# Linear attention in a fixed order, with paired products, gate products in between, and reordered weight loads

## The chip, the cores and the metric

The kernel runs on one core of one Trainium2 chip. The metric is the device time of one execution in microseconds (us); lower is better. A core has TensorE (PE, matmul; PEld is its weight load), VectorE (DVE), ScalarE (ACT), GpSimd (POOL), and SyncE (SP), whose queue issues all the loads that are spoken of here. Loads go from HBM into SBUF over 16 DMA engines; matmul results land in PSUM.

## What is computed

Two transformer blocks over 256 tokens of width 1024. The change lies in the first block, between its input projections and the routing of its mixture of experts (MoE). The part that matters of the reference:

```python
# two-directional gated linear attention: 4 heads, key width 128, value width 256, chunks of 64 tokens
cum = jnp.cumsum(la, axis=3); last = cum[:, :, :, -1:, :]
q_dec = qc * jnp.exp(cum); k_inv = kc * jnp.exp(-cum); k_rem = kc * jnp.exp(last - cum)
scores = jnp.where(lower, jnp.einsum('bhnid,bhnjd->bhnij', q_dec, k_inv), 0.0)
o_intra = jnp.einsum('bhnij,bhnjv->bhniv', scores, vc)
def step(state, inp):
    q_n, k_n, v_n, d_n = inp
    o_n = jnp.einsum('bhid,bhdv->bhiv', q_n, state)
    state = d_n[..., None] * state + jnp.einsum('bhid,bhiv->bhdv', k_n, v_n)
    return state, o_n
# forward, and backward over the flipped sequence; the start states come from a second sequence, ctx
ox = o_f + flip(o_b)
# mixer
o = _rmsnorm(o, gla_onorm_g)
y_gla = jnp.matmul(o * jax.nn.silu(g), w_gla_br)     # g: 1024 columns of the input projection w_in
gate_pool, gate_gla = jnp.split(jax.nn.sigmoid(gates), 2, axis=-1)
x = x + g1 * jnp.matmul(gate_pool * y_pool + gate_gla * y_gla, w_o)
# then 32 experts, two per token; then the second block (two attentions, two MLPs)
x = x + g2 * _hier_moe(...)
```

## The kernel before

The core works through the stages one after the other: projections of x and ctx, linear attention, the mixer with its gates, routing, the MoE with 192 weight tiles of 1 MB each, and the second block. Each dense product against a float32 weight is made of three products of split operands. `Chunk` loads a chunk of 1024 rows by 512 columns as two tiles of 1 MB (line 125) into a ring of three buffers named `raw`. `split` turns each chunk into four pieces `wsp`: ScalarE copies the high part (L243), VectorE subtracts it (L244). `mmB` then issues, for each group of 128 tokens (m), 24 matmuls of 512 columns (L283 to L285), so 48 for a chunk. There are four `wsp` buffers, so a chunk's piece is written when the last product on the former chunk's piece is done.

The linear attention is the loop `for hp in range(2)` over pairs of heads. For each pair it makes
- the start states of both directions from ctx (`krc` by `vc`, L578), copied by VectorE into `SS` (L581), which is the buffer F[4],
- the products inside the chunks (`scT` by `vx`, L587) into two PSUM tiles `po` with the tag "mm", of which there are four buffers,
- four steps. In each, for direction d, chunk n (n = step forward, 3 − step backward): the query product `qdec` by state `Sb(d, h)` (L596), with 64 output rows, which go to the upper or the lower half of a PSUM tile; the key-value product `krx` by `vx` (L603), which contracts over 64 rows; and the update of the state by VectorE (L607). Both directions' chunks lie in different halves of the 128 rows in every step. The last step has no key-value product and no update,
- the squares (L612, ScalarE), the root (L614, L166 to L176), and the scaling into `og` (L619, VectorE).

The chunk of `w_in` for g has two halves of 512 columns, called gate halves below. The loop `for h in range(2)` makes them; each half ends in a sigmoid (L153 to L155), a product by VectorE (L707) and one by GpSimd (L708). After them come the pool projection u, four chunks for `gates`, and the rest of the mixer.

Small products of the modulation vector ride along: `adaln_chunk` (L195) multiplies 1024 rows of `w_mod`, loaded by `wm_load` (L690) into buffers that are free by then (FA, XA, F[0], F[4]), in four column groups of 32; `adaln_T` (L213) and `adaln_bc` (L222) spread the result. `wm[4]` stands in FA and XA, `wm[5]` in F[0] and F[4].

`W.load` (L664) issues MoE tiles ahead. The first of them go into a pool "ring2" of seven buffers that lies where the work tiles of the attention (pool `fg`) were, so it must wait until these are done with.

The order on each engine: instructions outside of an `in_order` region are placed by a scheduler that simulates the engines; inside one, TensorE, ScalarE and VectorE keep the order of the code among themselves. From `sp.enter_context` on, SP's queue keeps the order of the code, too. Each engine works its own queue in order, and an instruction that waits holds up all behind it.

Of the kernel before, what the change touches and what calls it, by code (L numbers as in the profile page):

```python
# [13 lines left out]
AF = mybir.ActivationFunctionType  # L14
# [3 lines left out]
P = 128  # L18
# [3 lines left out]
NT = 2  # L22
# [65 lines left out]
def build(tc, I, out, dbg=None):  # L88
# [8 lines left out]
    with ExitStack() as top:  # L97
# [7 lines left out]
        def PS(tag="ps"):  # L105
            return psum.tile([P, 512], F32, name=tag, tag=tag)
# [243 lines left out]
        with b1:  # L350
# [217 lines left out]

            oss = fg.tile([P, 2, NT, 2], F32, name="oss")
            ors = fg.tile([P, 2, NT, 2], F32, name="ors")  # L570
            og = f3(F[2])
            for hp in range(2):
# [9 lines left out]
                po = []  # L582
                for m in range(NT):
                    po.append(PS("mm"))
                    for hh in range(2):
                        h = 2 * hp + hh
                        nc.tensor.matmul(po[m][:, hh * 256:(hh + 1) * 256], scT[0][m][:, h], vx[m][:, h * 256:(h + 1) * 256],  # L587
                                         start=(hh == 0), stop=False, skip_group_check=True)
                for step in range(4):
                    for d in range(2):  # L590
                        n = step if d == 0 else 3 - step
                        m, r = n // 2, n % 2
                        rsl = slice(64 * r, 64 * r + 64)
                        for hh in range(2):
                            h = 2 * hp + hh
                            nc.tensor.matmul(po[m][rsl, hh * 256:(hh + 1) * 256], qdec[d][:, h, n * 64:n * 64 + 64], Sb(d, h),  # L596
                                             start=False, stop=False, tile_position=(0, 64 * r), skip_group_check=True)
                        if step == 3:
                            continue
                        pkv = PS()  # L600
                        for hh in range(2):
                            h = 2 * hp + hh
                            nc.tensor.matmul(pkv[:, hh * 256:(hh + 1) * 256], krx[m][d][rsl, h * P:(h + 1) * P],  # L603
                                             vx[m][rsl, h * 256:(h + 1) * 256], start=True, stop=True, skip_group_check=True)
                        for hh in range(2):
                            h = 2 * hp + hh
                            nc.vector.scalar_tensor_tensor(Sb(d, h), Sb(d, h), dec[:, d, h, n:n + 1],  # L607
                                                           pkv[:, hh * 256:(hh + 1) * 256], op0=OP.mult, op1=OP.add)
                for m in range(NT):
                    for hh in range(2):  # L610
                        junk = fg.tile([P, 256], F32, name="aff", tag="aff", bufs=3)
                        nc.scalar.activation(junk, po[m][:, hh * 256:(hh + 1) * 256], AF.Square, accum_out=oss[:, hp, m, hh:hh + 1])  # L612
# [3 lines left out]
                for m in range(NT):  # L616
                    for hh in range(2):
                        h = 2 * hp + hh
                        nc.vector.tensor_scalar(og[:, m, h * 256:(h + 1) * 256], po[m][:, hh * 256:(hh + 1) * 256],  # L619
                                                ors[:, hp, m, hh:hh + 1], None, op0=OP.mult)  # L620

# [74 lines left out]
            for h in range(2):  # L696
                wg = Chunk(w_in, 2560 + h * 512)
                wm[4 + h] = wm_load(4 + h, *((FA, XA[0], XA[1]), (F[0], F[4]))[h])
                W.load(1)
                pg = denseC(wg, X)  # L700
# [11 lines left out]
            wg = Chunk(w_in, 0)  # L712
            wm[10] = wm_load(10, FA, F[4])
            W.load(1)
# [18 lines left out]
            for i in range(4):  # L733
# [3 lines left out]
                W.load(1)  # L737
# [977 lines left out]
```

## Time and profile before

| | us |
|---|---|
| median of three runs | 1460.36 (1458.88 to 1462.91) |
| the profiled execution | 1460.49 |
| its span in the profile | 1458.7 |
| TensorE busy in the span | 1275.9 (87%) |
| all MoE tiles | 192 loads of 1 MB |

The span leaves 1.8 us of the profiled execution outside. The profile has a row of tenths for each engine in 40 slices of 36.5 us, a row for the clock granted to TensorE (9 is nearly the whole of 2.4 GHz, a stretch at 0.5 ran at 1.2 GHz), and the share of the DMA engines. A float32 matmul of the program is two records in the trace, one of float32r is one. The end of a matmul is modelled; the start is measured. A busy TensorE is therefore not one at its peak, and the pitch of starts says more.

### The profile page before, as it was taken

How to read it: one execution, taken by the hardware profiler on the slowest of the kernel's cores; microseconds unless marked ns; L12 is line 12 of the kernel's file. 1: busy time of each engine (PE TensorE's matmuls, PEld its weight loads, DVE VectorE, ACT ScalarE, POOL GpSimd, SP SyncE). 2: the span in 40 equal slices, each digit the busy share in tenths (PEclk: the TensorE clock that was granted, in tenths of full speed). 3: DMA queues.
4: the chain of work that ended last, by engine and by line, in shares of the span. 5: the costliest groups of instructions: out<-in, count | busy, mean ns of one | idle time of the engine just before them, and what ended most of it. 6: DMA issues, size and time to landing. Idle time of an engine off the chain costs nothing.

```text
span 1458.7 us, 17343 instructions
## 1 busy us (share of the span) xinstructions
PE 1275.9 (87%) x7063; PEld 879.3 (60%) x7064; DVE 644.3 (44%) x978; ACT 481.0 (33%) x802; POOL 110.9 (8%) x57
## 2 busy tenths in 40 slices
PE   6899997999987776777777689999999998799997
PEld 4776755787732121221222167878999887688996
DVE  2543233457521120211201078675555765955554
ACT  3443104564410000000000066634445345444441
POOL 1100000000000000000000043030000320600000
PEclk9989998999998898998988899999999999999999
DMA  9822017955899999999999966146565450665650
GB/s 357 307 101 81 36 58 287 373 187 191 352 421 420 421 381 421 421 420 421 421 421 421 415 219 217 58 153 215 181 202 175 172 188 1 203 214 174 202 174 29
DMA packets 112672, 368.82 MB, mean 253 GB/s; under 512 B 7979, under 2 KB 9899, under 8 KB 88012
## 3 DMA queue, kind: packets, MB, share of 16 engines
q1 hardware_dynamic: 112588, 367.67, 66.3%
q8 instruction: 57, 0.93, 0.3%
q14 instruction: 27, 0.22, 0.0%
HBM read 366.60 MB, written 1.05 MB: 252 GB/s over the span
## 4 chain that ended last, share of the span: by engine, by line
PE 32%; DMA 22%; DVE 5%; ACT 2%; issue 1%; POOL 1%; SPq 0%; DVEq 0%; ACTq 0%; POOLq 0%
DMA raw<-in_moe_w_dram 21%; PE mm L285 7%; PE mm L284 6%; PE mm L283 6%; PE ps L299 3%; PE ps L298 3%; PE ps L297 3%; DVE wsp L244 2%; PE mm L1455 1%; DMA raw<-in_moba_w_qkv_dram 1%; DVE x L1318 1%; ACT wsp L243 1%; PE ps L1411 0%; DVE x L1321 0%; PE ps L1260 0%
## 5 line engine op out<-in xcount | busy, mean ns | idle before, releaser
L244 DVE TENSOR_TENSOR wsp<-raw,wsp 128x1024 fp32r<-128x1024 f32 (+1 forms) x208 | 260.5, 1267 | 180.8 <-ACT wsp L243 174.8
L243 ACT ACTIVATE wsp<-raw 128x1024 fp32r<-128x1024 f32 (+1 forms) x234 | 240.6, 1049 | 195.0 <-PE mm L285 69.8
L1057 PE MATMUL mm<-raw,XA 128*32 128x512 f32 x1024 | 190.4, 706 | 76.8 <-DMA raw<-in_moe_w_dram 73.6
L1057 PEld LDWEIGHTS mm<-raw,XA 128*32 128x32 f32 x1024 | 42.9, 125 | 218.8 <-DMA raw<-in_moe_w_dram 135.2
L244 POOL TENSOR_TENSOR wsp<-raw,wsp 128x1024 fp32r<-128x1024 f32 x26 | 65.8, 2553 | 783.1 <-PE ps L1106 469.7
L1073 DVE SCALAR_TENSOR_TENSOR t<-mm,w,t 128x512 f32<-128x512 f32 x8 | 8.9, 1112 | 255.3 <-PE mm L1057 215.3
L1057 PE MATMUL mm<-raw,t 128*32 128x512 f32 x512 | 86.4, 674 | 25.7 <-DMA raw<-in_moe_w_dram 23.3
L298 PE MATMUL ps<-hTl,wsp 128*128 128x256 f32 x384 | 108.7, 283 | 0.0
L299 PE MATMUL ps<-hTh,wsp 128*128 128x256 f32 x384 | 108.7, 283 | 0.0
L297 PE MATMUL ps<-hTh,wsp 128*128 128x256 f32 x384 | 108.6, 283 | 0.0
L283 PE MATMUL mm<-wsp,hh 128*128 128x512 f32 x240 | 93.8, 391 | 0.0
L284 PE MATMUL mm<-wsp,hh 128*128 128x512 f32 x240 | 93.6, 390 | 0.0
L285 PE MATMUL mm<-wsp,hl 128*128 128x512 f32 x240 | 93.3, 390 | 0.0
L284 PE MATMUL mm<-wsp,hTh 128*128 128x512 f32 (+1 forms) x224 | 86.9, 388 | 1.4 <-POOL wsp L244 1.4
L283 PE MATMUL mm<-wsp,hTh 128*128 128x512 f32 (+1 forms) x224 | 87.4, 390 | 0.0
L285 PE MATMUL mm<-wsp,hTl 128*128 128x512 f32 (+1 forms) x224 | 87.0, 389 | 0.0
L283 PE MATMUL mm<-wsp,R1h 128*128 128x512 f32 x176 | 70.8, 410 | 10.7 <-ACT wsp L243 10.7
L297 PEld LDWEIGHTS ps<-hTh,wsp 128*128 128x128 f32 x384 | 73.7, 192 | 0.6
L298 PEld LDWEIGHTS ps<-hTl,wsp 128*128 128x128 f32 x384 | 73.7, 192 | 0.5
L299 PEld LDWEIGHTS ps<-hTh,wsp 128*128 128x128 f32 x384 | 73.7, 192 | 0.1
L1057 PEld LDWEIGHTS mm<-raw,t 128*32 128x32 f32 x512 | 19.7, 121 | 87.3 <-DMA raw<-in_moe_w_dram 42.9
L284 PE MATMUL mm<-wsp,R1h 128*128 128x512 f32 x176 | 70.9, 405 | 1.4 <-DVE wsp L244 1.3
(390 smaller groups left out, 2088.0 us busy)
## 6 DMA issues: line engine op xcount, KB each, us to landing
raw<-in_moe_w_dram SPq DMA_DIRECT2D x192, 1024.0 KB, 19.8
raw<-in_mlp_w_in_dram SPq DMA_DIRECT2D x32, 1024.0 KB, 5.4
raw<-in_mlp_w_out_dram SPq DMA_DIRECT2D x32, 1024.0 KB, 5.3
raw<-in_w_in_dram SPq DMA_DIRECT2D x22, 1024.0 KB, 12.1
F<-in_w_mod_dram SPq DMA_DIRECT2D x16, 1024.0 KB, 11.0
raw<-in_moba_w_qkv_dram SPq DMA_DIRECT2D x12, 1024.0 KB, 7.2
raw<-in_dil_w_qkv_dram SPq DMA_DIRECT2D x8, 1024.0 KB, 5.2
FA<-in_w_mod_dram SPq DMA_DIRECT2D x4, 1024.0 KB, 12.5
```

The costliest lines, as they stand in the source:

```text
L243: nc.scalar.activation(hi, src, AF.Copy)
L244: eng.tensor_tensor(lo, src, hi.bitcast(F32), op=OP.subtract)
L283: nc.tensor.matmul(ps[:, :n], xh[:, k0 + k, sl], hi, start=(first and k == 0), stop=False)
L284: nc.tensor.matmul(ps[:, :n], xh[:, k0 + k, sl], lo, start=False, stop=False)
L285: nc.tensor.matmul(ps[:, :n], xl[:, k0 + k, sl], hi, start=False, stop=(last and k == e))
L297: nc.tensor.matmul(p, hi[:, fs], xh[:, k], start=a, stop=False, skip_group_check=True)
L298: nc.tensor.matmul(p, hi[:, fs], xl[:, k], start=False, stop=False, skip_group_check=True)
L299: nc.tensor.matmul(p, lo[:, fs], xh[:, k], start=False, stop=z, skip_group_check=True)
L1057: nc.tensor.matmul(ps[r], xs[:, r], ws(e), start=first, stop=last, tile_position=(0, CAP * e), skip_group_check=True)
L1073: nc.vector.scalar_tensor_tensor(self.hid.rearrange("p (j q) -> p q j", j=4), v(p3), self.w, v(s), op0=OP.mult, op1=OP.mult)
L1318: nc.vector.scalar_tensor_tensor(hs[n], hs[n], mv[:, 0:1], gb[:, n * 512:(n + 1) * 512], op0=OP.subtract, op1=OP.mult)
L1455: nc.tensor.matmul(po[:, m * S + i * 64:m * S + (i + 1) * 64], pTs[h0 + i][:, j * P:(j + 1) * P], v[:, kt, vs], start=(i == 0 and j == 0), ...
```

## The change

1. The loop over head pairs becomes functions (`states`, `inside`, `gla_step`, `squares`, `norms`), and one `in_order` region calls them in a written order.
2. `gla_step` makes the two directions' query products alternately (d = 0, d = 1, d = 0, d = 1), then their key-value products alternately, then the four updates.
3. The first gate half is loaded and split in this region, and its 48 products (`gate_step`, six at a time) stand between the steps. The second region, `for h in range(2)`, takes the finished `pg0` for h = 0.
4. The MoE tile that was issued after the first gate half's loads is not issued there; `W.load` is moved behind the second half's loads, and ahead of `wm[10]`'s. Chunks 1 and 2 of the four `gates` chunks issue two MoE tiles instead of one. The number issued up to the fourth chunk is seven, as before.

```diff
-            for hp in range(2):
+            wg = Chunk(w_in, 2560)
+            po, pg0 = {}, []
+            def states(hp):
...
-                for step in range(4):
-                    for d in range(2):
-                        n = step if d == 0 else 3 - step
...
+            def gla_step(hp, step):
+                at = [(n, n // 2, n % 2, slice(64 * (n % 2), 64 * (n % 2) + 64)) for n in (step, 3 - step)]
+                for hh in range(2):
+                    h = 2 * hp + hh
+                    for d, (n, m, r, rsl) in enumerate(at):
+                        nc.tensor.matmul(po[hp][m][rsl, hh * 256:(hh + 1) * 256], qdec[d][:, h, n * 64:n * 64 + 64], Sb(d, h),
+                                         start=False, stop=False, tile_position=(0, 64 * r), skip_group_check=True)
+                if step == 3:
+                    return
+                pkv = [PS() for _ in range(2)]
+                for hh in range(2):
+                    h = 2 * hp + hh
+                    for d, (n, m, r, rsl) in enumerate(at):
+                        nc.tensor.matmul(pkv[d][:, hh * 256:(hh + 1) * 256], krx[m][d][rsl, h * P:(h + 1) * P],
+                                         vx[m][rsl, h * 256:(h + 1) * 256], start=True, stop=True, skip_group_check=True)
+                for hh in range(2):
+                    h = 2 * hp + hh
+                    for d, (n, m, r, rsl) in enumerate(at):
+                        nc.vector.scalar_tensor_tensor(Sb(d, h), Sb(d, h), dec[:, d, h, n:n + 1],
+                                                       pkv[d][:, hh * 256:(hh + 1) * 256], op0=OP.mult, op1=OP.add)
...
+            def gate_step(m, step):
+                if step == 0:
+                    pg0.append(PS("mm"))
+                k = 2 * step
+                mmB(pg0[m], R1h, R1l, m, wg.wp[k:k + 2], first=(k == 0), last=(k == 6), k0=k)
+
+            with in_order():
+                states(0)
+                wg.split(2)
+                inside(0)
+                states(1)
+                for step in range(4):
+                    gla_step(0, step)
+                    if step in (0, 1):
+                        wg.split(1)
+                    if step < 3:
+                        gate_step(0, step)
+                squares(0)
+                norms(0)
+                gate_step(0, 3)
+                gate_step(1, 0)
+                gate_step(1, 1)
+                inside(1)
+                for step in range(4):
+                    gla_step(1, step)
+                    if step < 2:
+                        gate_step(1, step + 2)
+                squares(1)
+                norms(1)
...
             for h in range(2):
-                wg = Chunk(w_in, 2560 + h * 512)
+                if h:
+                    wg = Chunk(w_in, 2560 + h * 512)
                 wm[4 + h] = wm_load(4 + h, *((FA, XA[0], XA[1]), (F[0], F[4]))[h])
-                W.load(1)
-                pg = denseC(wg, X)
+                if h:
+                    W.load(1)
+                pg = denseC(wg, X) if h else pg0
...
             wg = Chunk(w_in, 0)
+            W.load(1)
             wm[10] = wm_load(10, FA, F[4])
-            W.load(1)
...
-                W.load(1)
+                W.load(1 if i in (0, 3) else 2)
```

On TensorE, in the first steps of the first head pair, these rows stand before (`ps` is the key-value PSUM tile, `mm` is a `po` tile, F3 and F5 hold `vx` and `krx`, F4 the states, QD the decayed queries):

```order
L603 MATMUL ps_1298<-F3_128,F5_130 128x256 x2
L596 MATMUL mm_1279<-F4_129,QD_132 64x256 x2
L603 MATMUL ps_1305<-F3_128,F5_130 128x256 x2
L596 MATMUL mm_1276<-F4_129,QD_132 64x256 x2
L603 MATMUL ps_1312<-F3_128,F5_130 128x256 x2
```

and in the first step of the first pair these now, with the first products of the gate half behind them:

```order
L600 MATMUL mm_1288<-F4_129,QD_132 64x256
L600 MATMUL mm_1289<-F4_129,QD_132 64x256
L600 MATMUL mm_1288<-F4_129,QD_132 64x256
L600 MATMUL mm_1289<-F4_129,QD_132 64x256
L608 MATMUL ps_1310<-F3_128,F5_130 128x256
L608 MATMUL ps_1311<-F3_128,F5_130 128x256
L608 MATMUL ps_1310<-F3_128,F5_130 128x256
L608 MATMUL ps_1311<-F3_128,F5_130 128x256
L283 MATMUL mm_1323<-wsp_1282,R1h_116 128x512
L284 MATMUL mm_1323<-wsp_1282,R1h_116 128x512
L285 MATMUL mm_1323<-wsp_1282,R1l_117 128x512
```

Before, two products of one direction stood together; now neighbours belong to the two directions, with another PSUM tile and the other half of the rows.

On SP, around the loads of the second gate half (`raw<-in_w_in_dram`), before:

```order
L690 DMA XA_124<-in_w_mod_dram 128x2x512
L664 DMA raw<-in_moe_w_dram 128x2048
L125 DMA raw<-in_w_in_dram 128x4x512 x2
L690 DMA F_125<-in_w_mod_dram 128x4x512
L690 DMA F_129<-in_w_mod_dram 128x4x512
L664 DMA raw<-in_moe_w_dram 128x2048
```

and now:

```order
L730 DMA XA_124<-in_w_mod_dram 128x2x512
L125 DMA raw<-in_w_in_dram 128x4x512 x2
L730 DMA F_125<-in_w_mod_dram 128x4x512
L730 DMA F_129<-in_w_mod_dram 128x4x512
L704 DMA raw<-in_moe_w_dram 128x2048
L125 DMA raw<-in_w_in_dram 128x4x512 x2
```

The second gate half's loads moved ahead of the first MoE tile. F_129 is F[4], which holds the states.

On TensorE, at the end of the attention, before (the 48 products of the second gate half stand between the first row and the second; F_125 and F_129 are F[0] and F[4], `wm[5]`):

```order
L222 MATMUL ps<-t_1521,selrow 128x512
...
L195 MATMUL ps<-F_125,cpad 32x512 x4
L195 MATMUL ps<-F_129,cpad 32x512 x4
```

and now, with the last query products of the attention ahead of them:

```order
L600 MATMUL mm<-F_129,QD 64x256 x4
L222 MATMUL ps<-t_1522,selrow 128x512
L195 MATMUL ps<-F_125,cpad 32x512 x4
L195 MATMUL ps<-F_129,cpad 32x512 x4
L283 MATMUL mm<-wsp,R1h 128x512
```

The products on `wm[5]` moved ahead of the second gate half's 48.

## Rows read from the trace of the kernel before

**Rows 1.** The page: TensorE's busy tenths and the DMA's, 40 slices.
```profile
PE   6899997999987776777777689999999998799997
DMA  9822017955899999999999966146565450665650
```
**Rows 2.** Stretches: start:end, length, busy us (records) per engine, granted clock, DMA share, GB/s.
```profile
166.20:226.30 60.10, 60.10 (x259) 37.31 (x258) 21.56 (x51) 9.39 (x29) 1.29 (x1) 0.97 0.10 36
226.30:235.60 9.30, 0.02 (x1) 0.00 (x0) 1.78 (x4) 2.13 (x4) 1.26 (x1) 0.67 0.82 302
235.60:250.70 15.10, 14.99 (x64) 10.43 (x64) 5.12 (x5) 4.46 (x6) 0.00 (x0) 0.86 1.04 391
250.70:371.50 120.80, 118.10 (x560) 92.10 (x557) 69.42 (x81) 66.14 (x96) 2.54 (x2) 1.00 0.67 244
533.00:836.00 303.00, 218.03 (x1158) 65.01 (x1156) 43.39 (x86) 16.78 (x36) 0.00 (x0) 0.89 1.01 421
```
**Rows 3.** The chain of work that ended last: first and last whole MoE pieces.
```profile
534.97 21.37 DMA raw<-in_moe_w_dram
...
816.47 19.84 DMA raw<-in_moe_w_dram
836.35 4.81 PE mm L1057 x21
```
**Rows 4.** Waits from 196 to 252: us in total, times, longest.
```profile
ACT wsp L243 <- DMA raw<-in_w_in_dram: 17.8, 3, 9.9
PE mm L283 <- ACT wsp L243: 9.4, 1, 9.4
```
**Rows 5.** SP's queue in order of time (start, us, what), and one wait of it.
```profile
195.33 1.01 SPq L690 DMA_DIRECT2D XA<-in_w_mod_dram  x2
226.97 0.34 SPq L664 DMA_DIRECT2D raw<-in_moe_w_dram  x1
227.36 0.98 SPq L125 DMA_DIRECT2D raw<-in_w_in_dram  x2
...
SPq L664 <- DVE F L619: 30.5, 1, 30.5
```
**Rows 6.** TensorE and ScalarE ahead of the attention, in order of time.
```profile
166.21 1.92 PE L195 MATMUL ps<-F,cpad 128*32 128x512 f32 x16
168.07 3.72 PE L587 MATMUL mm<-F,F 128*128 128x256 f32 x16
168.20 0.60 ACT L201 ACTIVATE t<-ps 128x512 f32<-128x512 f32 x1 [0.34 <-PE ps L195]
171.62 2.81 PE L213 MATMUL ps<-keep,t 128*128 128x2 f32 x16
174.30 5.39 PE L578 MATMUL ps<-XA,FA 128*128 128x256 f32 x16
```
**Rows 7.** TensorE and VectorE in the steps, in order of time.
```profile
181.70 1.13 PE L603 MATMUL ps<-F,F 64*128 64x256 f32 x4
182.75 1.08 PE L596 MATMUL mm<-F,QD 128*64 128x256 f32 x4
183.76 1.13 PE L603 MATMUL ps<-F,F 64*128 64x256 f32 x4
...
183.44 0.92 DVE L607 SCALAR_TENSOR_TENSOR F<-F,dec,ps 128x256 f32<-128x256 f32 x2 [1.15 <-PE mm L596]
```
**Rows 8.** Attention scores of the second block, two 64-row halves in turn.
```profile
897.89 1.03 PE L1411 MATMUL ps<-x,x 64*128 64x256 f32 x8
```
**Rows 9.** Stretches as in rows 2, around the changes of clock.
```profile
175.00:178.20 3.20, 3.20 (x9) 2.49 (x9) 0.65 (x1) 0.00 (x0) 0.00 (x0) 0.50 0.00 0
229.60:235.60 6.00, 0.00 (x0) 0.00 (x0) 0.00 (x0) 1.04 (x2) 0.00 (x0) 0.50 1.02 396
235.60:239.60 4.00, 3.89 (x8) 2.65 (x9) 3.60 (x4) 2.97 (x4) 0.00 (x0) 0.50 1.05 387
239.80:248.90 9.10, 9.10 (x44) 7.24 (x42) 0.92 (x1) 0.00 (x0) 0.00 (x0) 1.00 1.04 395
```
**Rows 10.** Loads issued from 194 to 196: KB each, median us to landing.
```profile
FA<-in_w_mod_dram SPq DMA_DIRECT2D x1, 1024.0 KB, 5.3
```
**Rows 11.** A split, the end of the second head pair, and L222, in order of time.
```profile
162.24 1.06 ACT L243 ACTIVATE wsp<-raw 128x1024 fp32r<-128x1024 f32 x1 [6.20 <-PE mm L285]
...
167.90 1.22 DVE L244 TENSOR_TENSOR wsp<-raw,wsp 128x1024 fp32r<-128x1024 f32 x1 [0.61 <-ACT wsp L243]
...
220.74 0.38 ACT L612 ACTIVATE aff<-mm 128x256 f32<-128x256 f32 x1 [0.23 <-PE mm L596]
...
225.14 1.66 DVE L619 TENSOR_SCALAR F<-mm,ors 128x256 f32<-128x256 f32 x4
...
254.44 1.02 PE L222 MATMUL ps<-t,selrow 128*128 128x512 f32 x2
254.89 0.80 PE L284 MATMUL mm<-wsp,R1h 128*128 128x512 f32 x1
```

More of the change, by code (lines that the diff above doesn't have):

```diff
@@ L581, in build, with inside @@
                     nc.vector.tensor_copy(SS[:, (d * 4 + 2 * hp) * 256:(d * 4 + 2 * hp + 2) * 256], pst)
-                po = []
+            def inside(hp):
+                po[hp] = [PS("mm") for _ in range(NT)]
                 for m in range(NT):
-                    po.append(PS("mm"))
                     for hh in range(2):
                         h = 2 * hp + hh
-                        nc.tensor.matmul(po[m][:, hh * 256:(hh + 1) * 256], scT[0][m][:, h], vx[m][:, h * 256:(h + 1) * 256],
+                        nc.tensor.matmul(po[hp][m][:, hh * 256:(hh + 1) * 256], scT[0][m][:, h], vx[m][:, h * 256:(h + 1) * 256],
@@ L588, in build @@
                                          start=(hh == 0), stop=False, skip_group_check=True)
-                for step in range(4):
-                    for d in range(2):
-                        n = step if d == 0 else 3 - step
[L592 to L608, printed above, removed]
@@ L609, in build, with squares @@
+            def squares(hp):
                 for m in range(NT):
@@ L611, in build, with norms @@
                         junk = fg.tile([P, 256], F32, name="aff", tag="aff", bufs=3)
-                        nc.scalar.activation(junk, po[m][:, hh * 256:(hh + 1) * 256], AF.Square, accum_out=oss[:, hp, m, hh:hh + 1])
+                        nc.scalar.activation(junk, po[hp][m][:, hh * 256:(hh + 1) * 256], AF.Square, accum_out=oss[:, hp, m, hh:hh + 1])
+            def norms(hp):
                 o4 = oss[:, hp].rearrange("p a b -> p (a b)")
@@ L618, in build @@
                         h = 2 * hp + hh
-                        nc.vector.tensor_scalar(og[:, m, h * 256:(h + 1) * 256], po[m][:, hh * 256:(hh + 1) * 256],
+                        nc.vector.tensor_scalar(og[:, m, h * 256:(h + 1) * 256], po[hp][m][:, hh * 256:(hh + 1) * 256],
                                                 ors[:, hp, m, hh:hh + 1], None, op0=OP.mult)
+            def gate_step(m, step):
[26 more added lines that the diff above has]
+                norms(1)
             pending = []
```

## The prediction

> **What bounds the kernel now.** I read the 40 slices first, then stretches of them, then waits. From the twelfth slice to the twenty-third the DMA engines are full while TensorE is not [rows 1]. From 533 to 836 us they carry 421 GB/s at a share of 1.01, and the chain of work that ended last runs through MoE tiles alone [rows 2, 3]. The number of MoE tiles, and of those issued ahead of that stage, is the same after the change. So what the change saves ahead of the MoE moves that stage and all behind it by as much, no more and no less. From 166 to 226 and from 250.7 to 371.5 TensorE is busy nearly throughout (60.1 of 60.1, 118.1 of 120.8 us) with the DMA at 0.10 and 0.67 [rows 2]: there TensorE's work is the bound. Between them lie 9.3 us in which it does nothing. Of these the waits say: the first product of the second gate half waits for ScalarE's copy, 9.4 us, and that copy waits for its tile [rows 4]. The tile is late because SP issued nothing from 196.3 to 226.97: the first MoE tile stood at the head of its queue and waited 30.5 us for the scaling L619, and the gate half's loads stood behind it [rows 5]. The time to predict is that from 168.07, when the last small product ahead of the attention is made [rows 6], to 250.7, where u's products begin [rows 2]: 82.6 us.
>
> **The change part by part: what it takes away.**
> 1. Pairing. A batch of two products of one direction, four records, takes 2.06 us per two batches (181.70 to 183.76), so 1.03 each [rows 7]. Two head pairs have 12 key-value and 16 query batches: 28 × 1.03 = 28.8. Whether the other half of the array can work meanwhile is shown elsewhere in this trace: eight records of the same 64-row shape, in alternating halves, take 1.03 too [rows 8]. For column halves no row has this shape; the nearest is the small product in four column groups, 16 records of 512 columns in 1.92 [rows 6], against 8 × 1.03 = 8.2 if one group ran after the other. So 14 batches remain: 14.4, **saved 14.4** (bounds 0 if nothing overlaps, 14.4).
> 2. The load wait: the second gate half's tiles are now issued when the start states are made, some 30 us before they are needed. **Saved 9.4**, with the gate half's weights split during the attention, by engines that have time (ScalarE 9.4 of 60 us busy, VectorE 21.6 [rows 2]).
> 3. The clock. After that idle time the granted clock was 0.5, and eight products took 4.0 us, the next forty 9.1 [rows 9]. 48 at the later pitch are 10.9; the stretch of 15.1 has them and a small product of 1.9 [rows 2, 6], so they took 13.2: **saved 2.3**.
>
> **What it adds.**
> 4. `wm[5]`'s second half goes into F[4], which holds the states, so its load can start only after the last query product; its product stands now ahead of the gate half's 48 on TensorE, where before it stood behind them. The load takes 5.3 us alone [rows 10], and the query batch's last product ends 0.4 after its start. Against these 5.8 (with 0.1 for the issue) TensorE has the rest of that batch, L222 (0.45 to the next start, 254.44 to 254.89 [rows 11]) and half of a small product (0.95): 1.7. **Cost 4.1.** Nothing else can go ahead of it, as the 48 stand behind it in the same queue. Bounds: 1, if the load lands as soon as TensorE gets there, and 7, if the gate half's loads are still in flight and it takes as long as under load.
> 5. The clock after that wait. Rows go both ways: the clock fell in the 9.3 us without work, and fell too after the 2.8 us of tiny products L213 (0.5 at 175.0 to 178.2), where 16 products then took 5.39 against 3.72 for as many of the same shape [rows 6, 9]. So 0 or 1.7; I take **0.9**.
> 6. L213 lost its cover. Before, L587's 16 products (3.6 us) stood between the small product and L213, while ScalarE copied the result (168.20 to 168.80). Now L213 comes next: **0.8**. Clock and length of the products behind stay.
> 7. `inside(1)` needs the two PSUM tiles of the first pair, which `norms(0)` gives back 6.1 us after the last query product (220.74 to 226.80 [rows 11]), or 5.3 without the sigmoid that stood between. 18 gate products (4.1) and part of the batch cover it: **0.5**. Behind it wait all of the second pair's products.
> 8. In each step VectorE makes four updates of 0.46, and they begin 0.69 after the batch whose first product they wait for (183.44 against 182.75 [rows 7]). So they are done 0.69 + 1.83 = 2.5 after the key-value batch begins; that batch and six gate products are 2.4 with a cut, so the next query batch finds them done, its second half with time to spare. TensorE's step is 1.03 + 1.03 + 1.4 + 0.15 = 3.6. Where VectorE has a split (1.22 [rows 11]) in its queue between updates, and that split waits for a `wsp` buffer that the gate products of the same step release, the next updates come 0.7 late. This happens in the second pair: **0.3**. Going from full-size to 64-wide products and back costs some 0.15 (a batch of four records takes 1.03, four of L587's sixteen in 3.6 us take 0.9 [rows 6, 7]). The gate products stand in five such cuts before and in six now, and a small product makes a seventh: **0.3**.
> 9. u's tiles. The first MoE tile still waits for the scaling of the second pair, and u's two tiles stand behind it. In the old order the scaling ends 6.1 after the last query product; the sigmoids of the first gate half (six of 0.63) now mix into that chain on ScalarE and may push it to 8. Then 5.3 for the MoE tile, 2.7 for u's first half at 391 GB/s, 1.1 for its copy: 15 to 17 after the last query product. TensorE is done with the gate half after 5.8 + 0.95 + 10.9 = 17.7. **0**, bounds 0 and 3.
> 10. From u on: the same products, and 3 MB that were carried after 227 are now carried before. Counted from the last query product, u's second tile lands at 17; then come five tiles of 2.7 up to the first `gates` chunk (at 28 and 31) and five up to the next (41 and 44). TensorE has u done, with a small product, at 31, and the next chunk, with the pool's products, at 45. So the first chunk's tiles land 3 us ahead, the next one's 4, less the 1.1 of the copy; behind that the lead grows, as two MoE tiles and two of a chunk are 10.8 against TensorE's 14. **0**, bounds 4, and a gain of the 2.7 us in which TensorE is idle there now [rows 2].
>
> The sum: 14.4 + 9.4 + 2.3 − 4.1 − 0.9 − 0.8 − 0.5 − 0.3 − 0.3 = 19.2. From the profiled 1460.5 (span 1458.7 and 1.8 around it, within 0.2 of the median) this gives 1441.3; placing every product in turn gave 18.4. I say **1441.5**. With items 4, 5, 9 and 10 at their ends the case's own range is 1435 to 1449.
>
> **A rule against it.** VectorE's four updates and a split are 1.83 + 1.22 = 3.05 us of a step in which TensorE's paired products are only 2.06 [rows 7, 11]. The Trainium skill, "TensorEngine Tiling (Array Packing)", section "PSUM Bottleneck", says that tiling makes TensorE faster but not the emptying of PSUM, which may then be the bound. By that rule the time is the second rival's below; by the rows the six gate products in each step cover it.
>
> **The rivals.**
> - The loads from 250.7 on also get out of the way and the small gaps go: 2.7 us more, and no fall of the clock: 1438. For it: the DMA ran at 1.04 until 290 or so. Against: 118.1 of 120.8 leaves little.
> - VectorE sets the step. If updates, split and the next query products follow each other without cover, a step is 1.03 + 0.69 + 1.83 + 1.22 = 4.8 with a split and 3.6 without, against 3.6 that I count. Four of the six steps have a split: 4.8, and two of the splits also push the updates behind them, by 1.2 each: 1448.5. For it: the splits stand in VectorE's fixed order between updates. Against: in the first pair these pieces were copied long before.
> - The pairs do not overlap, so the change doesn't do what it says there: 14.4 more, 1456. For it: no row with 64-column halves. Against: the scores of the second block [rows 8] and the four column groups [rows 6].
> - Slower: the clock. If the mixture of half-width products and waits keeps the granted clock at 0.5 through the eight steps and the gate products between them, their 26 us double: 1467.5. It turns slower than no change once more than 19 us of that work run at 0.5, and measurably so from some 24. For it: L213's tiny products, after which the clock fell [rows 9]. Against: the same 64-wide batches ran before at 0.97 on average of the whole stretch [rows 2], and now more stands between them.
>
> **How the numbers follow.** The forecast 0.61; more gained 0.08; VectorE 0.20; no overlap 0.07; the clock 0.04. About 0.3% (4.4 us) is what a measurement of this kernel can tell from no change, so below 1456.0 is faster: 0.61 + 0.08 + 0.20 = 0.89; within it 0.07; slower 0.04. The range must leave out at most 0.2: from 1435 to 1452 it holds the forecast, the larger gain and most of the VectorE case, some 0.85.
>
> **What would show it.** In the changed profile the query and key-value batches must be eight records in about 1.03 us; the 9.4 us wait for the gate half's tile must be gone; an idle time of some 4 us must stand before the product on F[4], with SP's wait for the last query product ahead of it; u's products must begin near 231.5 and the full DMA stretch 19 us earlier, near 352. I am wrong if u's first product waits for its tile, if the batches still take two times 1.03 for both directions, or if the stretch from u to the full DMA is longer than its 120.8 us.

## The result and the profile after

The changed kernel takes 1438.95 us (median of 4, 1437.89 to 1446.02) against 1460.03 before (median of 4, 1458.88 to 1462.91): a ratio of 0.9859, 95% interval 0.9835 to 0.9883, 21 us less. The profiled execution has a span of 1436.2 us against 1458.7.

Stretches of the changed kernel, columns as in [rows 2]: the attention from the small product of `wm[7]` to the last query batch, the wait that follows, the second gate half, u to the full DMA, and a piece of the MoE.

```profile
166.25:212.40 46.15, 45.43 (x257) 30.26 (x256) 24.77 (x48) 9.32 (x19) 0.00 (x0) 0.96 0.32 115
212.40:217.70 5.30, 2.13 (x12) 0.46 (x10) 2.58 (x6) 4.63 (x16) 0.72 (x1) 1.00 0.62 199
217.70:231.80 14.10, 14.06 (x58) 10.60 (x59) 5.28 (x9) 4.47 (x6) 3.06 (x3) 0.88 0.68 249
231.80:350.70 118.90, 117.06 (x556) 91.81 (x555) 68.20 (x80) 63.82 (x91) 1.29 (x1) 1.00 0.70 257
513.00:816.00 303.00, 217.40 (x1160) 64.56 (x1164) 43.41 (x86) 16.81 (x36) 0.00 (x0) 0.90 1.01 421
```

The 9.3 us hole of [rows 2] is a 3.2 us hole now, the DMA works during the attention (0.32 against 0.10), and u begins at 231.82 instead of 250.74. The MoE is the same 421 GB/s, only earlier: in the chain of work that ended last its final piece stands at 815.54 where it stood at 836.35 [rows 3], 20.8 us earlier.

```profile
795.67 19.83 DMA raw<-in_moe_w_dram
815.54 4.90 PE mm L1099 x21
```

TensorE in order of time (start, us, line; in brackets the idle time before and what ended it): ahead of the attention, one step, the end of the attention, the wait, and where u starts.

```profile
168.90 2.92 PE L213 MATMUL ps<-keep,t 128*128 128x2 f32 x16 [0.72 <-ACT t L201]
171.68 5.21 PE L582 MATMUL ps<-XA,FA 128*128 128x256 f32 x16
181.99 1.08 PE L600 MATMUL mm<-F,QD 128*64 128x256 f32 x8
183.00 1.13 PE L608 MATMUL ps<-F,F 64*128 64x256 f32 x8
185.67 1.08 PE L600 MATMUL mm<-F,QD 128*64 128x256 f32 x8
211.40 1.08 PE L600 MATMUL mm<-F,QD 128*64 128x256 f32 x8
212.41 1.13 PE L222 MATMUL ps<-t,selrow 128*128 128x512 f32 x2
213.47 1.06 PE L195 MATMUL ps<-F,cpad 128*32 128x512 f32 x8
217.74 1.07 PE L195 MATMUL ps<-F,cpad 128*32 128x512 f32 x8 [3.20 <-DMA F<-in_w_mod_dram]
218.73 0.50 PE L283 MATMUL mm<-wsp,R1h 128*128 128x512 f32 x1
220.30 0.63 PE L284 MATMUL mm<-wsp,R1h 128*128 128x512 f32 x1
231.36 1.02 PE L222 MATMUL ps<-t,selrow 128*128 128x512 f32 x2
231.82 1.03 PE L283 MATMUL mm<-wsp,R1h 128*128 128x512 f32 x2
```

Eight records of a query or key-value batch take what four took in [rows 7]; a step lasts 185.67 − 181.99 = 3.68 us. The product on F[4] waits 3.2 us, and the gate products behind it run at twice their time for some 3 us. SP's queue (columns as in [rows 5]) shows why it waits, and that the first MoE tile and u's tiles go out only at 221.5:

```profile
185.15 27.77 SPq L730 DMA_DIRECT2D F<-in_w_mod_dram  x2
221.48 0.34 SPq L704 DMA_DIRECT2D raw<-in_moe_w_dram  x1
221.87 0.98 SPq L125 DMA_DIRECT2D raw<-in_w_in_dram  x2
```

### The profile page after: what moved, and what is told of

Its sections match the earlier page's. It is cut to its first block, busy times and chain, and to the rows that moved or that the text cites. A ratio compares the mean times of both kernels' runs of the same rounds, so it can differ in the third digit from the quotient of the medians.

```text
span 1436.2 us, 17354 instructions
## 1 busy us (share of the span) xinstructions
PE 1260.8 (88%) x7063; PEld 872.3 (61%) x7064; DVE 644.9 (45%) x978; ACT 481.6 (34%) x802; POOL 111.0 (8%) x57
## 4 chain that ended last, share of the span: by engine, by line
PE 33%; DMA 23%; DVE 6%; ACT 2%; issue 1%; POOL 1%; SPq 0%; DVEq 0%; ACTq 0%; POOLq 0%
DMA raw<-in_moe_w_dram 22%; PE mm L285 7%; PE mm L284 6%; PE mm L283 6%; PE ps L299 3%; PE ps L298 3%; PE ps L297 3%; DVE wsp L244 2%; PE mm L1497 1%; DMA raw<-in_moba_w_qkv_dram 1%; DVE x L1360 1%; ACT wsp L243 1%; PE ps L1453 1%; DVE x L1363 0%; ACT pr L1471 0%
```

## The experiments

Single executions of one kernel lay up to 14 us apart in these runs; the last section shows a part of the reason. So each kernel is also read by two distances in its trace, both from the small product of `wm[7]` (166.25 in the changed kernel) as zero: to the first product of the pool, behind u, and to the last MoE product; and by what is left from there to the end of the span, where all kernels have the same work. Each ratio below is to the kernel before, measured beside that run; its median there was 1460.03 to 1461.15.

| kernel | median us (runs) | pool | last MoE | rest |
|---|---|---|---|---|
| before | 1460.03 (4) | 98.8 | 675.2 | 617.3 |
| changed | 1438.95 (4) | 78.8 | 654.4 | 615.5 |
| changed, once more | 1439.87 (4) | 80.3 | 655.7 | 621.0 |
| pairing undone | 1455.35 (10) | 92.5 | 672.3 | 620.7 |
| before, new loads only | 1453.58 (10) | 90.9 | 672.3 | 616.1 |
| MoE tile first again | 1461.88 (10) | 93.7 | 668.0 | 621.6 |
| no filler | 1443.26 (4) | 81.7 | 655.9 | 617.5 |
| wm[5] in F[1] | 1448.44 (6) | 78.6 | 660.0 | 620.5 |
| that, u's tiles first | 1436.31 (5) | 76.1 | 652.5 | 616.2 |
| the same, once more | 1435.35 (5) | 76.1 | 652.5 | 617.8 |
| that, early sigmoids | 1443.41 (6) | 74.5 | 655.3 | 622.2 |
| L213 moved | 1438.70 (6) | 76.3 | 655.2 | 620.7 |
| F[1], u first, L213 moved | 1438.95 (4) | 73.3 | 647.5 | 621.9 |

Theory throughout: the terms of the sum. Rivals: VectorE sets the step; the loads are hidden in either order; what is gained up to u is given back behind it.

**1. Pairing undone.**

```diff
-                for hh in range(2):
-                    h = 2 * hp + hh
-                    for d, (n, m, r, rsl) in enumerate(at):
+                for d in range(2):
+                    n = step if d == 0 else 3 - step
...
+                    for hh in range(2):
+                        h = 2 * hp + hh
```

The query products, the key-value products and the updates of one direction stand in one pass of the loop over d.

> The changed kernel with one part undone: within a step the products of one direction stand together again (its query batch, its key-value batch, its two updates, then the other direction's), in the same fixed order and with the same gate products between the steps. Theory (items 1 and 8: TensorE's own work sets the step, and two halves of the array work at once only when their products stand side by side): every batch of four records takes 1.03 us, the period of a step goes from 3.68 to about 5.7 us, and the kernel is 14 x 1.03 = 14.4 us slower than the changed one: about 1453.4. Rival (VectorE's updates and splits set the step, and the pairing itself is hidden): under the other direction's products the updates have more cover, so the step grows by less than half of that, and the time stays below 1447.

Measured: 1455.35, ratio to before 0.9956 (0.9935 to 0.9976). TensorE in one step, with the next step's start:

```profile
186.43 1.08 PE L602 MATMUL mm<-F,QD 128*64 128x256 f32 x4
187.44 1.13 PE L609 MATMUL ps<-F,F 64*128 64x256 f32 x4
190.09 1.08 PE L602 MATMUL mm<-F,QD 128*64 128x256 f32 x4
```

Each batch takes 1.03 us for one direction, and a step 5.72 instead of 3.68. From `wm[7]`'s product to the last query batch it is 57.49 us against 45.15: 12.3 more. The two last steps have no key-value batch, so there the two directions' query products stand side by side even here (eight in 1.09); 12 of the 14 batches were undone, 12 × 1.03 = 12.4. No wait for VectorE appeared in either kernel's steps. The theory holds; the expected 14.4 counted two batches too many for this kernel. The median is 16 us up (14 by the ratios), the pool 13.7 and the last MoE product 17.9. Over the first 235 us from zero the granted clock was 0.96 here and 0.98 in the changed kernel; 0.02 of 235 us is an estimate of some 5 us, which fits the 5.6 that come on top of 12.3, but it is not shown product by product.

**2 and 3. The loads alone, and the loads undone.** In the kernel before, the first MoE tile is put behind the second gate half's tiles and `wm[5]`, with the later MoE tiles as in the changed kernel; in the changed kernel, it is put ahead of them again.

```diff
-                W.load(1)
+                if h:
+                    W.load(1)
```

```diff
                 if h:
+                    W.load(1)
                     wg = Chunk(w_in, 2560 + h * 512)
...
-                if h:
-                    W.load(1)
```

> The kernel before with one part of the change alone: the loads in the new order (the first MoE tile behind the second gate half's tiles and wm[5], the later MoE tiles as in the changed kernel); the attention is written as before and its order is the scheduler's. Theory (items 2 and 3): the 9.4 us wait for the gate half's tile and the 2.3 us that the low clock costs behind it go, some 11 us: about 1449, with u's products near 239 to 240. Rival (loads and order only work together): the scheduler, which has the gate half's tiles early, puts its products ahead of the last query products, the scaling comes later and with it the first MoE tile and u's tiles, and less than 6 us are gained: above 1454.

> The changed kernel with one part undone: the first MoE tile stands ahead of the second gate half's tiles in SP's queue again, as before the change. Theory (items 2 to 4): the tile waits for the scaling of the second pair until about 221.4, and five tiles stand behind it up to wm[5]'s second half, whose product is ahead of the 48 on TensorE: they land at 2.7 us each, near 237; then 48 products at 10.9 to 13: u's products near 249, 17 to 18 us later, about 1456. Rival (TensorE's work sets the end of this stretch and the loads are hidden in either order): within 5 us of the changed kernel, below 1444.

Measured: the loads alone give 1453.58, ratio to before 0.9958 (0.9936 to 0.9980); undone, 1461.88, ratio 0.9999 (0.9981 to 1.0017): by the median no gain is left of the whole change. The kernel before with the new loads: VectorE's subtractions and its scaling, SP's queue, and u's first products:

```profile
225.15 4.17 DVE L244 TENSOR_TENSOR wsp<-raw,wsp 128x1024 fp32r<-128x1024 f32 x3 [0.34 <-ACT wsp L243]
231.90 1.66 DVE L619 TENSOR_SCALAR F<-mm,ors 128x256 f32<-128x256 f32 x4
233.65 0.34 SPq L664 DMA_DIRECT2D raw<-in_moe_w_dram  x1
243.10 0.73 PE L283 MATMUL mm<-wsp,R1h 128*128 128x512 f32 x2 [1.22 <-ACT wsp L243]
245.38 0.63 PE L283 MATMUL mm<-wsp,R1h 128*128 128x512 f32 x1
```

The changed kernel with the MoE tile first, the second gate half's first product:

```profile
230.74 1.22 PE L283 MATMUL mm<-wsp,R1h 128*128 128x512 f32 x2 [16.72 <-ACT wsp L243]
```

Alone, the loads bring u 9.0 us forward (75.5 us after `wm[7]`'s product against 84.5), near the 11 of the theory. But the copies and subtractions of the second gate half, whose tiles are early now, stand ahead of the scaling on ScalarE and VectorE. The scaling begins at 231.90 (before: 225.14 [rows 11], from a start 1.4 us earlier), the first MoE tile goes out at 233.65 (before: 226.97), u's tile is waited for 1.22 us, and the clock falls again (0.79 from 243 to 251): at the pool 7.9 are left, at the last MoE product 2.9, in the median 6.8. By the time that is near the rival: loads and order work together. The rival's reason was another, though: the last query product comes 53.8 us after `wm[7]`'s in both kernels, with gate products between the last batches in both.

Undone, the hole is 16.72 us, larger than the 9.4 of before, because TensorE runs out of work near 214 (before: 226.3) while the scaling, on which the MoE tile waits, comes only 5 us sooner (the tile goes out at 222.02 against 226.97). So about half of what the pairing saves becomes a longer wait. u begins at 246.71, where the theory had 249. This trace keeps some 5 us of the change at the pool and 7.2 at the last MoE product, and has 4.3 more in the rest; the median keeps nothing, and what took the remainder there is not shown. The doubled MoE tiles in the `gates` chunks (part 4 of the change) were not tried alone.

**4. No filler.** All 48 products of the first gate half stand behind the second pair.

```diff
-                    if step < 3:
-                        gate_step(0, step)
...
                 norms(1)
+                for m in range(NT):
+                    for step in range(4):
+                        gate_step(m, step)
```

> The changed kernel with one part undone: the 48 gate products stand behind the second pair, not between the steps and the pairs; the products stay paired and in fixed order. wm[5]'s second half then has the first gate half's 48 products ahead of it, so its wait (4.9 us with the clock behind it) goes. Theory (the filler hides VectorE's updates): a step needs its query batch (1.0), 1.2 to the first update, 0.8 for the first two, so about 3.1 to 3.4 us against 2.06 of products, and 1.2 more where a split stands between; the 36 products in the steps fill that, and 12 to 18 more cover the norms between the pairs. Without them 6 x 1.1 + 2.4 for two splits + 4 between the pairs come on top, 4.9 goes: about 1447. Rival (the filler hides nothing, TensorE's products follow each other anyway): 4.9 us faster, 1434.

Measured: 1443.26, ratio to before 0.9881 (0.9844 to 0.9917), between the two. One step:

```profile
187.09 1.13 PE L608 MATMUL ps<-F,F 64*128 64x256 f32 x8
188.79 1.82 PE L600 MATMUL mm<-F,QD 128*64 128x256 f32 x8 [0.57 <-DVE F L613]
```

The step is 3.45 us (its query batch begins at 185.34, the next one at 188.79), with 2.06 of products in it: TensorE waits 0.57 for the first update, and the query batch is stretched from 1.02 to 1.75 because each of its four products waits for its own update (they start 0.39 us apart, as the updates end). Here VectorE sets the step, and with six gate products in each it does not: 3.68 with 1.37 us of filler in it. The Trainium skill, "TensorEngine Tiling (Array Packing)", section "PSUM Bottleneck", says that tiling makes TensorE faster and not the emptying of PSUM; the step without filler agrees. Over the attention 10.9 us of gate products made it 45.15 − 40.64 = 4.5 longer, so 6.4 of them were hidden. The product on F[4] has the gate half as cover here and waits for nothing, which gives some of the 6.4 back. By the medians the kernel loses only some 4 us, and the two intervals overlap; at the last MoE product it is 1.5 us behind the one trace of the changed kernel and 0.2 behind the other. That the filler makes the whole kernel faster is therefore not shown, only that it hides VectorE's updates.

**5 and 6. The wait for F[4], and u's tiles.** First `wm[5]`'s second half goes into F[1], free from some 200 us on; then also u's tiles are issued ahead of the first MoE tile.

```diff
-                wm[4 + h] = wm_load(4 + h, *((FA, XA[0], XA[1]), (F[0], F[4]))[h])
+                wm[4 + h] = wm_load(4 + h, *((FA, XA[0], XA[1]), (F[0], F[1]))[h])
                 if h:
-                    W.load(1)
+                    wu = Chunk(w_in, 0)
                 pg = denseC(wg, X) if h else pg0
                 finish_adaln()
                 pending.append((gbc, 4 + h, adaln_chunk(wm[4 + h])))
+                if h:
+                    fgst.close()
+                    W.pool("ring2", 7)
+                    W.load(1)
```

> The changed kernel with one wait taken away: the second half of wm[5] goes into F[1], which is free once the second pair's inside products are made (about 200 us), and not into F[4], which is free only after the last query product (212.4). The first MoE tile and u's tiles stand where they stood in SP's queue. Theory A (items 4 and 5: the 3.2 us of idle time and the 1.7 us that the lower granted clock costs behind it lie on the path): both go, u's products begin near 226.9 and the time falls by 4.9 us to about 1434.0. Theory B (item 9: u's tiles land just in time as it is): they are still issued behind the first MoE tile, which waits for the scaling until about 221.4, and their first copy can't start before about 229.7; so TensorE waits there instead, u begins near 231, and at most 1 us is gained: about 1438.3.

> As the run with wm[5]'s second half in F[1], and u's two tiles now stand ahead of the first MoE tile in SP's queue. If theory B of that run is right, the two waits are removed together only here: u begins near 226.9, 4.9 us earlier, and the time is about 1434 to 1437 (the six tiles behind 221.5 take 2.7 us each, so the first gates chunk lands near 240 for a TensorE that wants it from 238.5 on, and up to 2.7 us may be given back). If theory A is right, it is the same as that run. If neither wait lay on the path, it stays at 1438.9.

> The kernel with wm[5]'s second half in F[1] and u's tiles ahead of the first MoE tile once more, beside the changed kernel on the same chip, because single executions of one kernel lay up to 10 us apart in the runs so far. Theory: 3 us faster than the changed kernel. Rival: the gain up to u (3.3 us) is given back behind it, and the two are within 1 us.

Measured: with F[1] alone 1448.44, ratio to before 0.9899 (0.9873 to 0.9925), slower than the changed kernel by the medians (the intervals overlap by 0.001); with u's tiles first 1436.31, ratio 0.9818 (0.9791 to 0.9846), and again 1435.35, ratio 0.9831 (0.9814 to 0.9848), where the changed kernel beside it had 1439.87 and 0.9857 (0.9840 to 0.9874). With F[1] alone, TensorE and ScalarE:

```profile
218.49 0.50 PE L283 MATMUL mm<-wsp,R1h 128*128 128x512 f32 x1 [1.51 <-DVE t L749]
231.43 2.01 ACT L243 ACTIVATE wsp<-raw 128x1024 fp32r<-128x1024 f32 x2 [5.22 <-DMA raw<-in_w_in_dram]
232.54 0.73 PE L283 MATMUL mm<-wsp,R1h 128*128 128x512 f32 x2 [1.99 <-ACT wsp L243]
248.10 0.73 PE L283 MATMUL mm<-wsp,R1h 128*128 128x512 f32 x2 [1.08 <-ACT wsp L243]
```

and the stretches behind its last two waits:

```profile
232.00:236.00 4.00, 2.93 (x12) 2.11 (x13) 3.39 (x4) 3.97 (x6) 0.00 (x0) 1.00 1.03 410
247.00:252.00 5.00, 3.44 (x11) 2.61 (x11) 3.92 (x4) 4.80 (x8) 0.00 (x0) 0.74 1.06 395
```

The wait for F[4] is gone, and two others stand behind it: 1.5 us for the PSUM tile that the first gate half's sigmoid gives back, and 2.5 for u's tile, as theory B said. Then 1.1 for the first `gates` chunk. At the last MoE product it is 5.6 behind the changed kernel, and 5.0 more lie in the rest, not more than between the changed kernel's own two traces (615.5 and 621.0); B's 1438.3 is too low by 10. Up to the pool this kernel is 0.2 us ahead, so the 5.6 arise behind it. The first two waits were not followed by a lower clock (1.00 from 218 to 222 and from 232 to 236), the third was (0.74 from 247 to 252, where the changed kernel has 1.00). The clock fell twice more on the way to the first MoE product (0.83 from 315 to 325, 0.57 from 375 to 380), in the changed kernel once (0.92 from 356 to 378); why there is not shown. With u's tiles loaded during the attention no tile is waited for at u, the pool is reached 2.7 us sooner and the last MoE product 2.0. This version has the lowest medians: 4.5 us ahead of the changed kernel by those beside each other, though the two intervals overlap a little.

**7 to 9. Early sigmoids, and the tiny products moved.** On top of the last kernel, the first gate half's sigmoids stand in the second pair's steps; in the changed kernel, L213's 16 products of `wm[7]` stand in the first pair's steps; and that together with F[1] and u's tiles first.

```diff
+                    if step in (1, 2):
+                        gate_sig(step - 1)
...
+                    if step in (1, 2):
+                        adaln_T(1 + 2 * step, 7, part, step == 2)
```

`gate_sig(m)` is the sigmoid of pg0[m] and its product with it.

> As the run with wm[5]'s second half in F[1] and u's tiles ahead of the first MoE tile, and the sigmoids of the first gate half with their products stand in the second and third step of the second pair, not behind its squares. In that run the second gate half's first product waited 1.5 us for a PSUM tile that the product of the first gate half's sigmoid gives back. Theory: this wait goes, and the squares no longer share ScalarE with the sigmoids, so u's products come 1.5 us earlier than there: about 1434.8. Rival (behind u the loads set the time, the DMA share is 1.03 there): it is given back in the gates chunks and the time stays at about 1436.3.

> The changed kernel with the tiny products of wm[7] (L213, 16 of them) moved from the place ahead of the start states into the first pair's steps: eight behind the gate products of the second step, eight behind the third's. Theory (items 5 and 6: they cost 0.7 us because nothing stands between them and ScalarE's copy, and the granted clock of 0.69 behind them costs the next 16 products 1.4): both go, about 1436.9, and the 16 products of the start states take 3.6 us. Rival (the clock falls behind these products wherever they stand): the 16 take 3.6, but products in or behind the steps take twice their time, and 0.7 us or less is left: 1438.2 or more.

> The two edits that gained time up to u's products, together: wm[5]'s second half in F[1] with u's tiles ahead of the first MoE tile, and the tiny products L213 of wm[7] in the first pair's steps. Theory: they are worth 3.3 us (clock and wait at F[4]) and some 2.5 us (L213 and the clock behind it) up to u's first product, which would begin near 226 after the same start; and since u's tiles are there and the scaling, the first MoE tile and the first gates chunk come 2.5 us earlier too, no tile is waited for behind u as it was in the run with L213 alone: about 2.5 us faster than the kernel with the first edit alone. Rival: the loads behind u set the time, and no more than 0.5 us is left of L213's gain.

> The changed kernel itself, beside the two others: its time should be near 1439 again, and the stretch from the first product of wm[7] to u's first product 65.6 us long.

Measured: 1443.41 (0.9867, 0.9836 to 0.9898), 1438.70 (0.9847, 0.9818 to 0.9875), 1438.95 (0.9859, 0.9842 to 0.9876), and the changed kernel itself 1439.87; its stretch to u was 67.0 us, not 65.6, by the clock behind F[4]'s wait. The early sigmoids gain 1.6 us up to the pool, near the expected 1.5, but the median is 7 us above that of the kernel without them, which neither forecast had: the scheduler put ten gate products ahead of the last query batch and more inside it, so that the scaling came late and the first MoE tile went out at 229.38; by the first MoE product the gain was gone (2.5 us behind). Here, the second of three groups of that batch, and SP:

```profile
216.95 0.65 PE L600 MATMUL mm<-F,QD 128*64 128x256 f32 x4
229.38 0.82 SPq L713 DMA_DIRECT2D raw<-in_moe_w_dram  x2
```

With L213 moved, the start states take 3.6 instead of 5.0 and u begins 2.5 us sooner; then the first `gates` chunk is waited for, and the clock falls to 0.64 from 246 to 250, so that the time is the rival's although the products behaved as in the theory:

```profile
168.83 3.72 PE L583 MATMUL ps<-XA,FA 128*128 128x256 f32 x16
245.09 0.73 PE L283 MATMUL mm<-wsp,R1h 128*128 128x512 f32 x2 [1.08 <-ACT wsp L243]
246.00:250.00 4.00, 3.70 (x13) 3.06 (x14) 4.00 (x5) 2.78 (x5) 0.00 (x0) 0.64 1.05 424
```

Together with u's tiles first the gain survives up to the last MoE product, 7.0 us ahead of the changed kernel and 5.0 ahead of the one with F[1] and u's tiles first. Yet the time is about that of the changed kernel and 3.6 us above the latter's beside it, where 2.5 less were expected: in the profiled execution the rest of the span took 621.9 us, in the other two 615.5 and 617.8.

## Why the prediction was right, point by point

Forecast 1441.5, measured 1438.95, inside the case's own range of 1435 to 1449. u was to begin near 231.5 and began at 231.82; the full DMA was to come 19 us earlier and came 20.8 earlier (350.7 against 371.5). Items 1 to 8 as measured add up to 20.0 us, and u came 19.0 earlier, counted from the small product of `wm[7]` (65.6 us against 84.5); a small product that now stands ahead of u (L222, 0.46) is half of that difference, the other half is not assigned.

1. Pairing, 14.4: right. 14 batches of eight records in 1.01 to 1.07; the column halves, for which no row stood, behave as the row halves do; experiment 1 gives 1.03 for each batch.
2. and 3. The gate half's tile and its clock, 9.4 and 2.3: both are gone in the changed kernel. Experiments 2 and 3 show what the sum did not say: these terms are not the loads' alone. Without the fixed order a quarter (2.9 us at the last MoE product) to three fifths (6.8 in the median) of them is left, and without the loads the wait grows by 7.4 us.
4. The wait for F[4], 4.1: 3.2 (3.3 to 3.4 in three other traces). The load was issued at 212.55 and 217.74 − 212.55 = 5.2, issue included, where the sum had 5.8 with the rest of the batch.
5. The clock behind it, 0.9: mis-sized. The 48 products took 231.36 − 218.73 = 12.6 us instead of 10.9, so 1.7; 2.9 in the changed kernel's second trace. Of the two values that I halved between, 0 and 1.7, it was the upper one. Items 4 and 5 together were 5.0 in the sum and 4.9 in the trace: the one was too large and the other too small by nearly as much, which is luck.
6. L213 without cover, 0.8: 0.72.
7. `inside(1)` and the norms, 0.5: no wait. VectorE's scalings of `norms(0)` ran from 197.22 to 198.88 and gave the first tile back before `inside(1)` began at 198.26.
8. VectorE and the cuts, 0.6: 6 × (3.68 − 3.6) = 0.5. The parts were otherwise. Updates begin 1.17 us after the batch (184.17 against 183.00), not 0.69: the row that 0.69 was read from waits for a query product, these wait for the key-value batch. The splits pushed nothing.
9. u's tiles, 0 with bounds 0 and 3: no wait before u's first product, and none behind it (its first two products start 0.64 us apart, as in the kernel whose u tiles are early). The scaling ended 8.9 us after the last query batch (221.39 against 212.48), later than the 8 I allowed; TensorE was later too, by item 5. Experiment 5 shows how thin that was: 2.5 us of wait once F[4]'s was out of the way.
10. From u on, 0 with a gain of up to 2.7: mis-sized, 1.9 gained, most of the 2.5 by which the forecast was too high. TensorE idles 1.84 us there instead of 2.70, and a small product (L222, 0.46) stands ahead of u now; the rest, some 0.6, is in pieces too small to name.

The rivals. Loads out of the way: its 2.7 us came for the most part, its clock fall stayed; by time it was nearer than the forecast (1438 and 1441.5 around 1438.95). VectorE sets the step: not with the filler, and experiment 4 shows that it would without. No overlap: out, by the first trace. The clock at 0.5 through the steps: out, 1.00 from 182 to 212.

## What to carry to other kernels

A saving ahead of a full-DMA stretch counts only if the loads at the head of the in-order DMA queue come forward with it: the whole change was worth 21 us, and with the old load order nothing of it was left in the median, some 5 us up to the pool. Work that depends on nothing, put between dependent batches, hid 6.4 of its 10.9 us, in an order that was fixed by hand; where the scheduler was free it put other work ahead of what released the next loads (ahead of the scaling in experiment 2, of the last query batch with the early sigmoids). Before removing a wait, look for the one that would end next: behind F[4] stood a PSUM tile and u's tile, and it paid only when those were early too.

## What the runs showed of the hardware that was not expected

**The same work, 6.7 us apart.** The span behind the last MoE product has the same instructions in all kernels and took 615.5 to 622.2 us. The chain of the changed kernel, and of the one with F[1], u's tiles first and L213 moved, shows the same 48 products of the second block's local attention:

```profile
1202.96 5.31 PE mm L1497 x48
```

```profile
1198.65 9.26 PE mm L1501 x48
```

and the changed kernel once more, the same program in another execution:

```profile
1204.57 10.13 PE mm L1497 x48
```

Their stretches, in the same order:

```profile
1205.00:1210.00 5.00, 5.00 (x46) 5.00 (x46) 3.72 (x11) 1.17 (x2) 0.00 (x0) 1.00 0.00 2
```

```profile
1200.00:1205.00 5.00, 5.00 (x26) 5.00 (x25) 2.20 (x9) 1.65 (x4) 0.00 (x0) 0.50 0.01 2
```

```profile
1205.00:1210.00 5.00, 5.00 (x25) 5.00 (x25) 2.25 (x10) 2.31 (x8) 0.00 (x0) 0.50 0.00 2
```

Ahead of these products TensorE had gaps in all three (busy 7.86 of the 10 us from 1195 in the first, 3.57 of the 5 us from 1195 in the second, 7.81 of the 10 us from 1195 in the third). In the first the granted clock stayed at 1.00; in the other two it fell to 0.5, its lower level of 1.2 GHz. So no edit is needed for the difference, and what decides is not shown. In the thirteen traces these products took 5.31 us seven times, with a rest of 615.5 to 620.5 us, and 8.95 to 10.13 us six times, with a rest of 620.7 to 622.2. That is why distances inside the trace are compared here, not medians alone.

**GpSimd holds VectorE.** VectorE and GpSimd in the changed kernel, between the squares and the scaling of the second pair:

```profile
217.36 0.91 DVE L174 TENSOR_TENSOR rst<-rsy,rst 128x4 f32<-128x4 f32 x1
218.30 1.20 DVE L175 TENSOR_TENSOR rst<-rsy,rst 128x4 f32<-128x4 f32 x1
219.53 0.16 DVE L176 SCALAR_TENSOR_TENSOR ors<-rst,rsy 128x4 f32<-128x4 f32 x1
216.98 2.51 POOL L750 TENSOR_TENSOR F<-F,t 128x512 f32<-128x512 f32 x2 [78.70 <-DVE t L749]
```

Products of 128 x 4 that take 0.16 us elsewhere (L175 in the kernel before) take 0.91 and 1.20 beside two of GpSimd's and end when those end: 1.8 us on the chain to the first MoE tile and u's tiles. The 6.1 us that item 9 took from the old order held 0.6 of it (L174 took 0.77 there, beside one of GpSimd's), so 1.2 are new. The Trainium skill, "SBUF — State Buffer", section "Who interferes with whom", says that a VectorE instruction with two SBUF inputs contends with a GpSimd one that reads SBUF; this trace agrees.
